# A hybrid streaming-encoder block on one core: heads spaced further apart, one gate projection moved ahead of the first norm, small blocks moved to GpSimd, weight sums pinned

## The chip, the core and the metric

The kernel runs on one core of a Trainium2 chip. The metric is the device time of one execution in microseconds (us). An engine's name in the profile stands for: PE the matrix engine TensorE (PEld its weight loads), DVE VectorE, ACT ScalarE, POOL GpSimd, SP SyncE, which here only starts transfers.

## What is computed

One layer of a hybrid block on 512 frames of 1024 channels, in float32:

```python
h = rmsnorm(x, norm1_w[l])
proj = h @ w_in[l]
q, k, v, z, b_raw, a_raw, glu, gates = jnp.split(proj, SPLITS, axis=-1)
...
beta = jax.nn.sigmoid(b_raw.astype(jnp.float32))
g = -jnp.exp(dn_A_log[l].astype(jnp.float32)) * jax.nn.softplus(
    a_raw.astype(jnp.float32) + dn_dt_bias[l].astype(jnp.float32))
o = gated_delta_rule_chunked(q, k, v, g, beta).astype(x.dtype)
o = rmsnorm(o, dn_norm_w[l]) * jax.nn.silu(z.reshape(B, T, DN_HEADS, DN_HEAD_DIM))
out_a = o.reshape(B, T, DN_WIDTH) @ dn_w_o[l]
...
c = causal_depthwise_conv(c, cm_dw_w[l]) + cm_dw_b[l]
c = jax.nn.silu(layernorm(c, cm_ln_w[l], cm_ln_b[l]))
out_b = c @ cm_w_pw2[l] + cm_b_pw2[l]
...
x = x + (gate_a * out_a + gate_b * out_b) @ w_out[l]
h2 = rmsnorm(x, norm2_w[l])
f_gate, f_up = jnp.split(h2 @ ffn_w_gate_up[l], 2, axis=-1)
x = x + (jax.nn.silu(f_gate) * f_up) @ ffn_w_down[l]
```

q, k and v go through a 4-tap causal convolution and silu, c is a gated linear unit followed by a 31-tap one, and the delta rule solves a triangular system in each chunk, for 8 heads of 128 channels.

## The kernel before

**Products.** Every weight arrives as float32 (`raw`) and is split in two: ScalarE rounds it to `whi` (L107) and VectorE subtracts to get `wlo` (L108). The data are split the same way (`hh` and `hl`, `yh` and `yl`, and so on). A product is then three matrix products, hh·whi, hl·whi and hh·wlo (`split3`, L117). A column unit of 128 columns takes 8 steps of k, 24 products of 512 columns. The 64 units of the input projection, and those of the later projections, pass through three weight buffers (`unit`, L97).

**Start.** SyncE starts the transfers one after another: the vectors `vec`, then quarter by quarter the inputs `xt` and quarters of three weight units, with the small weights of beta and alpha (`wba`, L228) behind the first inputs. The first three units (two for the first gated linear unit, one for the second) and the products for beta and alpha (L263, L264) are made from `uh` and `ul`, the input times the norm's weight, split, not yet divided by the root mean square. The result is multiplied by the reciprocal root, `rsb`, afterwards. Only then come the normalized `hh` and `hl` (L297, L298), on which all later projections work. VectorE then turns alpha into the decays `g` (L316 to L333), in small steps.

**Heads.** Python generators lay out the program. `step()` takes the next step from a queue of `head(h)` and `take(8)`: a head is its four projections k, q, v and z, one step for each k; `take` does eight steps of `others()`, the gated linear units and then the 16 gates. So heads are 40 steps apart. Besides, `chains` hold work that advances when the step count allows: `decays()` (the four matrix products L699 that sum g within chunks, and L706), each head's second half, and, from step 84 on every 40 steps, the chain of one head, in which small products, R (L547) and w (L552) go back and forth between TensorE, VectorE and ScalarE. `front(h)` prepares it: GpSimd multiplies `Un` by the decay `DT` (L420). The diagonal blocks of 32x32 are copied out as `cp` by ScalarE (four copies, L425), and combined to 16x16 blocks `cc` by ScalarE (L427) and VectorE (L428). `cc` is written to memory and read back spread out as `U`. GpSimd makes `Ud` (L437) and inverts the blocks in 15 rounds of two small instructions (L446, L448). `finish` (L589, L590) transposes a head's output and multiplies it by silu of z.

The 31-tap convolution is 240 VectorE instructions (L612) of low priority, emitted every 40 steps. `behind()` and `issue_after` hold an instruction back in its engine's order until marked ones of other work have been issued; within these rules a scheduler orders each engine's instructions.

**Fill work.** Sums of weight blocks for the feed-forward (Strassen-like products) are made beside the rest: transfers that accumulate, started by GpSimd, and GpSimd additions on halves of blocks (`dsums_add`, L167, in the tiles U, wsh, wst).

**After the heads.** The output projection splits the heads' results (L799, L800) and multiplies by `wo`. Within it stand the layer norm's mean (L631) and, three units later, its norm (L647). In between VectorE subtracts the mean, ScalarE squares and GpSimd adds the squares (L642). Then follow the point-wise projection, the merge and `w_out`, the second norm, and transposes of its result (L902) into hh and hl (L904, L905), 128 frames at a time. The first three feed-forward units begin with 256 of the 512 frames, before the last transposes (`norm2`, L886 to L892). Feed-forward up and down follow. In the down projection `two` (L1119) adds finished partial sums from a list `left`, one at each k.

## Time and profile before

| | us |
|---|---|
| median of three runs | 975.80 |
| lowest, highest | 973.53, 977.41 |
| the profiled execution | 975.02 |
| its span in the trace | 973.2 |
| TensorE busy | 942.7 |
| VectorE busy | 730.4 |
| ScalarE busy | 537.9 |
| GpSimd busy | 347.9 |

A row of the timeline gives start, duration, engine, line, operation, output and inputs, shape and count, and in brackets how long the engine was idle before it and what it then waited for. A row of waits gives engine, operation and releaser, then the total, the number and the longest of such waits. A row of a group gives busy time and mean length in ns, then the idle time before it. A row of windows gives the stretch, its length, and the busy time and number of instructions of PE, PEld, DVE, ACT and POOL, then the granted clock, the share of DMA and GB/s. Records of matrix products overlap, so the time that one takes is read from the distance of two starts.

### The profile page before, as it was taken

The page shows a single profiled execution, that of the slowest core. Times are in us where ns is not written, and L with a number is a line of the kernel's source. Part 1 is how long each engine was busy: PE and PEld are TensorE (multiplying, and loading weights), DVE is VectorE, ACT ScalarE, POOL GpSimd, SP SyncE. Part 2 cuts the span into 40 slices and gives each one's busy share as a digit, 9 for nine tenths or more (in the row PEclk, how much of TensorE's full clock was granted, in tenths as well). Part 3 has the DMA queues.
Part 4 walks back from the last instruction along what each step waited for, and adds up shares of the span by engine and source line. Part 5 has one row for each costly group of instructions (what it writes and reads, how often), then busy time and mean ns, then how long its engine had stood idle before and what let it go on. Part 6 is the DMA issues. An engine that isn't in the chain of part 4 may idle for free. (4 is left out here: it accounts for less than half of the span.)

```text
span 973.2 us, 14887 instructions
## 1 busy us (share of the span) xinstructions
PE 942.7 (97%) x5199; PEld 795.3 (82%) x5199; DVE 730.4 (75%) x1125; ACT 537.9 (55%) x1130; POOL 347.9 (36%) x516
## 2 busy tenths in 40 slices
PE   7999999999999999999998999999999999999996
PEld 5687878878787888888886888888889999988875
DVE  4898988878888868889667753666434787789775
ACT  6688768678767573543536332333323554556544
POOL 0314524424252345254253442254441111134225
PEclk9999999999999999999999999999999999999998
DMA  8233422313222247688987985488899656577654
GB/s 316 86 128 100 142 78 66 99 44 122 81 84 89 76 132 217 180 258 286 299 253 233 272 254 162 174 242 281 282 266 222 205 174 196 171 225 246 225 180 143
DMA packets 78300, 177.40 MB, mean 182 GB/s; under 512 B 10209, under 2 KB 19329, under 8 KB 77201
## 3 DMA queue, kind: packets, MB, share of 16 engines
q1 hardware_dynamic: 66816, 144.88, 44.7%
q0 software_dynamic: 10256, 28.89, 12.9%
q10 hardware_dynamic: 1152, 2.69, 0.7%
q8 instruction: 41, 0.67, 0.3%
q14 instruction: 35, 0.28, 0.1%
HBM read 156.22 MB, written 45.37 MB: 207 GB/s over the span
## 5 line engine op out<-in xcount | busy, mean ns | idle before, releaser
L107 ACT ACTIVATE whi<-raw 128x1024 fp32r<-128x1024 f32 (+1 forms) x191 | 196.2, 1029 | 253.4 <-PE mm L117 154.3
L108 DVE TENSOR_TENSOR wlo<-raw,whi 128x1024 fp32r<-128x1024 f32 (+1 forms) x191 | 239.6, 1255 | 93.8 <-ACT whi L107 92.7
L117 PE MATMUL mm<-hh,whi 128*128 128x512 f32 (+1 forms) x688 | 269.5, 392 | 0.0
L117 PE MATMUL mm<-hl,whi 128*128 128x512 f32 (+1 forms) x688 | 263.5, 383 | 2.3 <-POOL hl L298 1.7
L117 PE MATMUL mm<-hh,wlo 128*128 128x512 f32 (+1 forms) x688 | 264.7, 385 | 0.5 <-DVE wlo L108 0.5
L612 DVE SCALAR_TENSOR_TENSOR cps<-c,c31w,cps 128x512 f32<-128x512 f32 x240 | 180.0, 750 | 5.7 <-ACT cps L610 1.6
L117 PEld LDWEIGHTS mm<-hl,whi 128*128 128x128 f32 x688 | 129.9, 189 | 24.7 <-POOL hl L298 2.9
L117 PEld LDWEIGHTS mm<-hh,wlo 128*128 128x128 f32 x688 | 129.6, 188 | 24.3 <-DVE wlo L108 0.9
L117 PEld LDWEIGHTS mm<-hh,whi 128*128 128x128 f32 x688 | 129.8, 189 | 21.0 <-ACT hh L297 0.2
L939 POOL TENSOR_TENSOR fm<-fm 128x256 f32<-128x256 f32 x33 | 30.1, 914 | 113.7 <-DVE s L939 91.9
L446 POOL TENSOR_TENSOR ytm<-U,y 128x60 f32<-128x60 f32 (+14 forms) x120 | 37.4, 311 | 53.3 <-DMA U<-sc 39.0
L370 DVE SCALAR_TENSOR_TENSOR acc<-mm,c4w,acc 128x511 f32<-128x511 f32 (+2 forms) x72 | 53.0, 738 | 2.1 <-ACT acc L367 1.7
L117 PE MATMUL mm<-yh,whi 128*128 128x512 f32 x128 | 51.3, 401 | 0.0
L117 PE MATMUL mm<-yh,wlo 128*128 128x512 f32 x128 | 50.5, 395 | 0.0
L117 PE MATMUL mm<-yl,whi 128*128 128x512 f32 x128 | 50.3, 393 | 0.0
L117 PE MATMUL w<-hl,whi 128*128 128x256 f32 x168 | 47.5, 283 | 1.1 <-DVE hl L905 1.1
L117 PE MATMUL w<-hh,wlo 128*128 128x256 f32 x168 | 47.6, 284 | 0.8 <-DVE wlo L108 0.8
L117 PE MATMUL w<-hh,whi 128*128 128x256 f32 x168 | 47.3, 284 | 0.2 <-ACT hh L904 0.2
L117 PE MATMUL w<-wlo,fh 128*128 128x512 f32 (+1 forms) x115 | 44.5, 387 | 0.6 <-DVE wlo L108 0.6
L117 PE MATMUL w<-whi,fl 128*128 128x512 f32 (+1 forms) x115 | 44.2, 385 | 0.0
L117 PE MATMUL w<-whi,fh 128*128 128x512 f32 (+1 forms) x115 | 44.2, 384 | 0.0
L191 POOL DMA_DIRECT2D s<-in_wgu_dram x24 | 22.6, 957 | 54.4 <-DMA s<-in_wgu_dram 54.4
(320 smaller groups left out, 1912.5 us busy)
## 6 DMA issues: line engine op xcount, KB each, us to landing
raw<-in_win_dram SPq DMA_DIRECT2D x61, 512.0 KB, 3.5
raw<-in_wgu_dram SPq DMA_DIRECT2D x32, 512.0 KB, 3.6
s<-in_wgu_dram SPq DMA_DIRECT2D x48, 256.0 KB, 5.7
raw<-s SPq DMA_DIRECT2D x48, 256.0 KB, 3.5
raw<-wsum SPq DMA_DIRECT2D x44, 256.0 KB, 4.2
raw<-in_wdn_dram SPq DMA_DIRECT2D x33, 256.0 KB, 4.1
s<-in_wgu_dram POOLq DMA_DIRECT2D x24, 256.0 KB, 6.6
s<-s POOLq DMA_DIRECT2D x24, 256.0 KB, 6.6
```

The costliest lines, as they stand in the source:

```text
L107: marked(S.activation(hi, raw, AF.Copy), "unit")
L108: marked(V.tensor_tensor(out=lo, in0=raw, in1=hi.bitcast(F32), op=ALU.subtract), "unit")
L117: marked(PE.matmul(ps, l, r, start=first and i == 0, stop=last and i == 2))
L191: fed.append(nc.gpsimd.dma_start(*begun.pop(0), accum_op=ALU.add, max_dma_last_dim=2048))
L370: marked(V.scalar_tensor_tensor(out=acc[:, s:], in0=ps[:, :T - s], scalar=c4w[:, j, k:k + 1], in1=acc[:, s:], op0=ALU.mult, op1=ALU.add))
L446: G.tensor_tensor(out=tm[:, :, 0:w], in0=U[:, k, :, k + 1:], in1=y[:, :, k:k + 1].broadcast_to([P, NT, w]), op=ALU.mult)
L612: V.scalar_tensor_tensor(out=acc, in0=c[:, k:k + T], scalar=c31w[:, i, k:k + 1], in1=acc, op0=ALU.mult, op1=ALU.add)
L939: return eng.tensor_tensor(out=out, in0=in0, in1=in1, op=op)
```

## The change

The line numbers of the kernel after are 1 to 22 higher. The core of the diff:

```diff
+OTHERS = (12, 12, 12, 12, 8, 8, 8, 8)
...
     def dsums_add(k, r, cs=slice(0, T)):
...
+        with tc.issue_after(last[0].ins):
+            for o, x, y in ((b22, b12, b22), (b12, b11, b12), (b11, b22, b11), (b21, b11, b21)):
+                G.tensor_tensor(out=o, in0=x, in1=y, op=ALU.add)
...
-        nc.sync.dma_start(vec, a["vec"])
+        nc.scalar.dma_start(vec, a["vec"])
...
+            for u in (1, 2):
+                load(u, q)
             if q == 0:
                 nc.sync.dma_start(wb, a["wba"])
-            for u in (1, 2):
-                load(u, q)
...
+            if k == 1:
+                V.tensor_copy(out=wbh, in_=wb)
+                V.tensor_tensor(out=wbl, in0=wb, in1=wbh.bitcast(F32), op=ALU.subtract)
+            for b in [k - 2] if 1 < k < KD - 1 else [k - 2, k - 1, k] if k > 1 else []:
+                PE.matmul(bps[0:32, :], wbs[:, 32 * b:32 * b + 32], uh[:, b, :], start=b == 0, stop=False)
+                PE.matmul(bps[0:16, :], wbs[:, 32 * b:32 * b + 16], ul[:, b, :], start=False, stop=b == KD - 1)
...
+        zps = pst.tile([P, 4, P], F32, name="st").rearrange("p n t -> p (n t)")
+        hi, lo = unit(a["win"][24])
+        for k in range(KD):
+            c = slice(k * P, k * P + P)
+            split3(zps, (hi[:, c], lo[:, c]), uh[:, k, :], ul[:, k, :], k == 0, k == KD - 1)
...
+        with tc.issue_after(g_.ins):
+            V.tensor_tensor(out=zall[:, 0, :], in0=zps, in1=rsb, op=ALU.mult)
+        S.activation(zall[:, 0, :], zall[:, 0, :], AF.Silu)
...
-        DT = gp.tile([P, NT, P], F32, name="DT", bufs=2)
+        DT = gp.tile([P, NT, P], F32, name="DT", bufs=3)
...
-            S.copy(out=cp[b32], in_=Un[b32, :, b32])
...
+            (G.tensor_copy if h else S.copy)(out=cp[b32], in_=Un[b32, :, b32])
+        if h:
+            G.tensor_scalar(out=cc, in0=cp[:, :, 0:16], scalar1=mh1, scalar2=None, op0=ALU.mult)
+            G.tensor_scalar(out=cp[:, :, 0:16], in0=cp[:, :, 16:32], scalar1=mh2, scalar2=None, op0=ALU.mult)
+            c_ = G.tensor_tensor(out=cc, in0=cc, in1=cp[:, :, 0:16], op=ALU.add)
...
+        with tc.issue_after(c_.ins) if h else nullcontext():
+            G.tensor_tensor(out=Ud, in0=Un, in1=mc.rearrange("p (a t) -> p a t", a=1).broadcast_to([P, NT, P]),
+                            op=ALU.mult)
...
-            if count[0] % ROUND == 0:
+            if count[0] % 8 == 0:
                 background()
...
-        yield 2
+        yield 6
...
+        if h:
+            pz = yield from proj(24 + h)
+            S.activation(z_, pz, AF.Silu)
...
-        chains.append([count[0] + 5, second()])
+        chains.append([count[0] + (5 if h else 13), second()])
...
-        queue.append(take(8))
+        queue.append(take(OTHERS[h] if h else 8 + OTHERS[0]))
...
-        if nh < H and count[0] >= START + ROUND * nh:
+        if nh < H and count[0] >= START + 32 * nh + sum(OTHERS[:nh]):
...
-                for ps, w in first:
+                for ps, w in first[:2]:
                     k_loop(ps, w, slice(0, 2 * P))
-                transposes(3)
+                with tc.issue_after(transposes(3).ins):
+                    k_loop(*first[2], slice(0, 2 * P))
...
-            if left:
+            if left and k % 2:
                 with behind():
                     left.pop(0)()
```

In words. The vectors are loaded by ScalarE's queue, the small weights after the first three weight quarters, and the products for beta and alpha trail the projection by two steps of k. Head 0's z projection is made in the start stage from uh and ul, into the bank that the chains use later, and scaled by rsb behind g. Heads stand 44 steps apart four times, then 40; head 0 takes 20 steps of others in place of its z. The blocks of heads 1 to 7 are copied, scaled and added by GpSimd. The weight sums' additions stand behind the last of the small inversions, or of the squares' sums, that has been laid out before them (`last[0]`). The last transposes stand before the third of the half loops. In the down projection `left` is taken up at odd k only. The convolution's taps are emitted every 8 steps.

TensorE's order around the first normalized projections, before: `b` is the last early unit, `g<-cst,cv` the transposes of beta and alpha (L306), `mm<-hh` and `mm<-hl` the first normalized ones.

```order
L117 MATMUL b<-uh,whi 128x512
L117 MATMUL b<-ul,whi 128x512
L117 MATMUL b<-uh,wlo 128x512
L306 MATMUL g<-cst,cv 128x32 x4
L117 MATMUL mm<-hh,whi 128x512
L117 MATMUL mm<-hl,whi 128x512
L117 MATMUL mm<-hh,wlo 128x512
```

After, 24 products into the bank `st` stand between the two; here are the last of them.

```order
L118 MATMUL st<-uh,whi 128x512
L118 MATMUL st<-ul,whi 128x512
L118 MATMUL st<-uh,wlo 128x512
L318 MATMUL g<-cst,cv 128x32 x4
L118 MATMUL mm<-hh,whi 128x512
L118 MATMUL mm<-hl,whi 128x512
```

The decays' products (L699, now L719) come 90 products behind L306 in before, and 59 behind L318 in after.

TensorE's order where the heads end, before: the transposes of head 7's output (`b<-cst,o`) are followed by further gates' products.

```order
L117 MATMUL mm<-hh,wlo 128x512
L383 MATMUL b<-cst,o 128x128 x4
L117 MATMUL mm<-hh,whi 128x512
L117 MATMUL mm<-hl,whi 128x512
L117 MATMUL mm<-hh,wlo 128x512
```

After, the output projection's (`yh`, `yl`) follow at once, with the layer norm's mean (L651) among the first.

```order
L118 MATMUL mm<-hh,wlo 128x512
L397 MATMUL b<-cst,o 128x128 x4
L118 MATMUL mm<-yh,whi 128x512 x2
L651 MATMUL mm<-sacc,cst 128x512
L118 MATMUL mm<-yl,whi 128x512
L118 MATMUL mm<-yh,wlo 128x512
```

Of the 72 products between transposes and output projection none is left; between mean and norm there are now 119 where there were 73.

GpSimd's order around the squares' sums (`sacc`), before: a weight sum in the tile `wsh` and its transfer stand ahead.

```order
L167 TENSOR_TENSOR wsh<-wsh 128x256 x4
L168 DMA wsum<-wsh 512x1x256
L191 DMA s_127<-s_125 128x512
L642 TENSOR_TENSOR sacc<-sacc,acc_5220 128x512
L642 TENSOR_TENSOR sacc<-sacc,acc_5224 128x512
```

After, the first `wsh` sum stands behind the last square.

```order
L193 DMA s_125<-s_124 128x512
L662 TENSOR_TENSOR sacc<-sacc,acc_5221 128x512
L662 TENSOR_TENSOR sacc<-sacc,acc_5225 128x512
L662 TENSOR_TENSOR sacc<-sacc,acc_5229 128x512
L662 TENSOR_TENSOR sacc<-sacc,acc_5233 128x512
L662 TENSOR_TENSOR sacc<-sacc,acc_5237 128x512
L662 TENSOR_TENSOR sacc<-sacc,acc_5241 128x512
L662 TENSOR_TENSOR sacc<-sacc,acc_5245 128x512
L193 DMA s_124<-in_wgu_dram 128x512
L169 TENSOR_TENSOR wsh<-wsh 128x256 x4
```

More of the change, by code (lines that the diff above doesn't have):

```diff
@@ L165, in dsums_add @@
         b11, b12, b21, b22 = (r[:, i, :] for i in range(4))
-        for o, x, y in ((b22, b12, b22), (b12, b11, b12), (b11, b22, b11), (b21, b11, b21)):
-            G.tensor_tensor(out=o, in0=x, in1=y, op=ALU.add)
+        with tc.issue_after(last[0].ins):
+            for o, x, y in ((b22, b12, b22), (b12, b11, b12), (b11, b22, b11), (b21, b11, b21)):
+                G.tensor_tensor(out=o, in0=x, in1=y, op=ALU.add)
         nc.gpsimd.dma_start(wsum[k][:, :, cs], r)
@@ L243, in block_kernel @@
         wbh, wbl = wbhl[:, :, 0, :], wbhl[:, :, 1, :]
-        V.tensor_copy(out=wbh, in_=wb)
-        V.tensor_tensor(out=wbl, in0=wb, in1=wbh.bitcast(F32), op=ALU.subtract)
         bps = psg.tile([P, T], F32, name="g")
@@ L262, in block_kernel @@
                 split3(ps, (hi[:, c], lo[:, c]), uh[:, k, :], ul[:, k, :], k == 0, k == KD - 1)
-            PE.matmul(bps[0:32, :], wbs[:, 32 * k:32 * k + 32], uh[:, k, :], start=k == 0, stop=False)
-            PE.matmul(bps[0:16, :], wbs[:, 32 * k:32 * k + 16], ul[:, k, :], start=False, stop=k == KD - 1)
+            if k == 1:
[4 more added lines that the diff above has]
+                PE.matmul(bps[0:16, :], wbs[:, 32 * b:32 * b + 16], ul[:, b, :], start=False, stop=b == KD - 1)
         ss = st.tile([P, 2, NT], F32, name="rms_ss", bufs=1)
@@ L281, in block_kernel @@
             split3(eps_[3], (hi[:, c], lo[:, c]), uh[:, k, :], ul[:, k, :], k == 0, k == KD - 1)
+        zps = pst.tile([P, 4, P], F32, name="st").rearrange("p n t -> p (n t)")
[3 more added lines that the diff above has]
+            split3(zps, (hi[:, c], lo[:, c]), uh[:, k, :], ul[:, k, :], k == 0, k == KD - 1)
+        zall = pa_.tile([P, H, T], F32, name="A")
         def glu0(i):
@@ L332, in block_kernel @@
         V.scalar_tensor_tensor(out=sp, in0=ax, scalar=0.0, in1=sp, op0=ALU.max, op1=ALU.add)
-        V.tensor_tensor(out=g, in0=sp, in1=nea.rearrange("p (a h) -> p a h", a=1).broadcast_to([P, NT, H]),
+        g_ = V.tensor_tensor(out=g, in0=sp, in1=nea.rearrange("p (a h) -> p a h", a=1).broadcast_to([P, NT, H]),
                         op=ALU.mult)
@@ L375, in conv4 @@
         return o
-    zall = pa_.tile([P, H, T], F32, name="A")
     junk = tp.tile([P, T], F32, name="pa", bufs=1)
@@ L422, in front @@
         cp = gp.tile([P, NT, 32], F32, name="cp")
+        cc = gp.tile([P, NT, 16], F32, name="cc")
         for b in range(4):
             b32 = slice(32 * b, 32 * b + 32)
-            S.copy(out=cp[b32], in_=Un[b32, :, b32])
-        cc = gp.tile([P, NT, 16], F32, name="cc")
-        S.activation(cc, cp[:, :, 0:16], AF.Copy, scale=mh1)
-        V.scalar_tensor_tensor(out=cc, in0=cp[:, :, 16:32], scalar=mh2, in1=cc, op0=ALU.mult, op1=ALU.add)
+            (G.tensor_copy if h else S.copy)(out=cp[b32], in_=Un[b32, :, b32])
[3 more added lines that the diff above has]
+            c_ = G.tensor_tensor(out=cc, in0=cc, in1=cp[:, :, 0:16], op=ALU.add)
+        else:
+            S.activation(cc, cp[:, :, 0:16], AF.Copy, scale=mh1)
+            V.scalar_tensor_tensor(out=cc, in0=cp[:, :, 16:32], scalar=mh2, in1=cc, op0=ALU.mult, op1=ALU.add)
         sc = dram.tile([8, 16, NT, 16], F32, name="sc")
@@ L436, in front @@
         Ud = gp.tile([P, NT, P], F32, name="Ud", bufs=3)
-        G.tensor_tensor(out=Ud, in0=Un, in1=mc.rearrange("p (a t) -> p a t", a=1).broadcast_to([P, NT, P]),
-                        op=ALU.mult)
+        with tc.issue_after(c_.ins) if h else nullcontext():
+            G.tensor_tensor(out=Ud, in0=Un, in1=mc.rearrange("p (a t) -> p a t", a=1).broadcast_to([P, NT, P]),
+                            op=ALU.mult)
         y = gp.tile([P, NT, 16], F32, name="y", bufs=3)
@@ L728, in head @@
         v_ = yield from v
-        pz = yield from proj(24 + h)
         z_ = zall[:, h, :]
-        S.activation(z_, pz, AF.Silu)
+        if h:
+            pz = yield from proj(24 + h)
+            S.activation(z_, pz, AF.Silu)
         def second():
@@ L901, in transposes @@
                     k = 4 * j + c
-                    PE.transpose(ps[:, c, :], xs2[:, n, k * P:(k + 1) * P], ident)
+                    t = PE.transpose(ps[:, c, :], xs2[:, n, k * P:(k + 1) * P], ident)
             k4 = slice(4 * j, 4 * j + 4)
             S.activation(hh[:, k4, ts], ps, AF.Copy)
-            V.tensor_tensor(out=hl[:, k4, ts], in0=ps, in1=hh[:, k4, ts].bitcast(F32), op=ALU.subtract)
+            marked(V.tensor_tensor(out=hl[:, k4, ts], in0=ps, in1=hh[:, k4, ts].bitcast(F32), op=ALU.subtract), "hl")
+        return t
     first = []
```

## The prediction

> **What bounds the kernel now.** I read the page's busy times first, then TensorE's waits by releaser, then the timeline around each wait.

> ```profile
> PE 942.7 (97%) x5199; PEld 795.3 (82%) x5199; DVE 730.4 (75%) x1125; ACT 537.9 (55%) x1130; POOL 347.9 (36%) x516
> ...
> PE mm L647 <- POOL sacc L642: 3.5, 1, 3.5
> PE st L555 <- ACT w L552: 3.2, 4, 1.1
> ...
> PE g L383 <- ACT Vp L456: 1.0, 1, 1.0
> PE st L550 <- DVE R L547: 1.0, 1, 1.0
> ```

> TensorE is busy 97% of the 973.2 us span: it is the bound, and every other engine matters only where TensorE waits for it. The rows behind the first give total, number and longest of such waits. The change takes no matrix product away, so the most it can win is waiting and slow clock. Two pairs of neighbouring rows give the price of a 512-column product at either clock, as the distance of their starts:

> ```profile
> 506.42 0.39 PE L117 MATMUL mm<-yh,wlo 128*128 128x512 f32 x1
> 506.65 0.39 PE L117 MATMUL mm<-yh,whi 128*128 128x512 f32 x1
> ...
> 518.17 0.63 PE L117 MATMUL mm<-yh,whi 128*128 128x512 f32 x1
> 518.60 0.63 PE L117 MATMUL mm<-yl,whi 128*128 128x512 f32 x1
> ```

> So 0.23 us at the full clock (0.2275 over longer rows) and 0.43 at the slow one. I sum against the profiled execution, 975.0 us (its span and 1.8 around it); the runs' median, 975.8, lies 0.8 above it.

> **1. Start: −1.1 us (−0.7 to −1.5).**

> ```profile
> 0.73 0.39 SPq L216 DMA_DIRECT2D vec<-in_vec_dram  x1
> 1.17 0.42 SPq L224 DMA_DIRECT2D xt<-in_xt_dram  x1
> ...
> 7.07 0.61 PE L263 MATMUL g<-uh,cv 128*32 128x512 f32 x1 [7.07 <-DVE cv L245]
> ```

> The first product is one of beta/alpha, and it waits for the small weights' split. With vec on ScalarE's queue SyncE issues every input one slot (0.44 us) earlier, and the first product becomes one of the projection, which needs only xt and a weight quarter. Both rows together say it can start at about 5.95 instead of 7.07. The small weights come in behind the quarters, and their products trail by two k, so nothing waits for them. The lower end is the slot alone and some of the DVE step, the upper one has the weight quarter a slot earlier as well.

> **2. Un-normalized gate ahead of the normalized inputs: −3.0 (−2.5 to −3.9).**

> ```profile
> 36.00:46.00 10.00, 7.68 (x31) 5.03 (x31) 9.94 (x13) 4.56 (x8) 6.02 (x4) 1.00 0.00 0
> ...
> 40.37 0.50 PE L117 MATMUL mm<-hl,whi 128*128 128x512 f32 x1 [1.29 <-POOL hl L298]
> 45.32 0.50 PE L117 MATMUL mm<-hl,whi 128*128 128x512 f32 x1 [0.36 <-POOL hl L298]
> ```

> Between 36 and 46 us TensorE issues 31 products, 31 × 0.2275 = 7.05 us of work in 10: 2.95 lost waiting for hh and hl, which DVE (9.94 of 10 busy) makes no faster. Head 0's z now fills 24 × 0.2275 = 5.46 us ahead of it. The last hl, used at 45.3, is ready a microsecond earlier (its chain starts with part 1) and wanted at about 45.5, so none of these waits stays. The upper end leaves the 0.36; the lower adds what falls outside the window. The z products are no extra: they leave head 0's later steps.

> **3. A new wait in its place, at the decay products: +2.6 (0 to +4.3).** They stood behind 90 products of the first projections, and now stand behind 59. The window is DVE's from the first step behind hl to g (L333), which they need:

> ```profile
> 44.95:59.98 15.03, 14.67 (x65) 12.12 (x65) 13.95 (x33) 12.38 (x18) 2.72 (x9) 1.00 0.34 113
> ...
> L370 DVE SCALAR_TENSOR_TENSOR acc<-mm,c4w,acc 128x511 f32<-128x511 f32 (+2 forms) x8 | 5.8, 719 | 0.2 <-ACT acc L367 0.2
> L108 DVE TENSOR_TENSOR wlo<-raw,whi 128x1024 fp32r<-128x1024 f32 x4 | 4.9, 1220 | 0.2 <-ACT whi L107 0.2
> L612 DVE SCALAR_TENSOR_TENSOR cps<-c,c31w,cps 128x512 f32<-128x512 f32 x3 | 2.2, 744 | 0.0
> ...
> 59.88 0.18 DVE L333 TENSOR_TENSOR cv<-cv 128x32 f32<-128x32 f32 x1
> 60.45 0.97 PE L699 MATMUL g<-cv,cst 128*128 128x32 f32 x8
> ```

> The first projection starts at about 36.1 − 1.1 + 5.5 = 40.5, so TensorE is at the decays at 40.5 + 59 × 0.2275 = 53.9. DVE comes to the window's start 1.1 earlier, at 43.85. Of its 13.95 us of work it now does, ahead of g, three 4-tap steps and one split less and two 31-tap steps more: 13.95 − 3 × 0.72 − 1.22 + 2 × 0.74 = 12.05. That is 55.9, with g itself 56.1, and 0.4 from its end to TensorE (60.06 to 60.45): TensorE starts them at 56.5, 2.6 late. All projections of head 0 queue behind, so this is lost outright. The high end adds the window's own idle time, 1.1, and as much again of the 12.38 ScalarE is busy with; the low end is DVE in time.

> **4. 16x16 blocks on GpSimd: −5.0 (0 to −6.5).** Around one of the six waits of the heads' chains (the three last rows of the first fence: 3.2 + 1.0 + 1.0 = 5.2 us):

> ```profile
> 259.96 1.22 ACT L425 COPY cp<-Un 32x128 f32<-32x128 f32 x4 [0.63 <-POOL Un L420]
> ...
> 262.21 0.28 DVE L428 SCALAR_TENSOR_TENSOR cc<-cp,cst,cc 128x64 f32<-128x64 f32 x1 [1.37 <-ACT cc L427]
> 262.81 0.49 PE L550 MATMUL st<-R,Y 128*128 128x128 f32 x2 [0.98 <-DVE R L547]
> ...
> L446 POOL TENSOR_TENSOR ytm<-U,y x120: 208/256/1314, 87.6 to 365.0; 128x60 f32<-128x60 f32 x8, 128x56 f32<-128x56 f32 x8, 128x52 f32<-128x52 f32 x8, 128x48 f32<-128x48 f32 x8
> ```

> ScalarE stops for GpSimd's Un, copies, and DVE stops 1.37 us for ScalarE; behind them in both queues stand another head's chain steps, R and w, and TensorE waits for these. With the blocks on GpSimd neither queue stops there. I take 5.0 of the 5.2; the low end adds the fill and drain around each, the high end is that the queues stop for something else. GpSimd pays 7 heads × 7 instructions × 0.3 us (the row's median is 0.26 for the nearest size) = 15 us, hidden: it is 36% busy. Its own pinning of Ud delays nothing TensorE asks for soon. The wider spacing (44 steps four times, then 40) and the third decay buffer move products among each other at no price, ±1.

> **5. The end of head 7: +1.8 (+1.0 to +5.5).**

> ```profile
> 466.53 0.60 PE L383 MATMUL b<-cst,o 128*128 128x128 f32 x4
> 467.17 0.75 DVE L590 SCALAR_TENSOR_TENSOR A<-b,vec,A 128x512 f32<-128x512 f32 x1
> 467.84 1.21 DVE L108 TENSOR_TENSOR wlo<-raw,whi 128x1024 fp32r<-128x1024 f32 x1
> 469.50 4.28 ACT L799 ACTIVATE yh<-A 128x512 fp32r<-128x512 f32 x8 [1.36 <-issue]
> 470.16 4.90 DVE L800 TENSOR_TENSOR yl<-A,yh 128x512 fp32r<-128x512 f32 x8 [1.11 <-ACT yh L799]
> ```

> Before, 72 products (16.4 us) stand between head 7's transposes and the first product of the output projection. The later chains leave none: two yh products, the layer norm's mean, then one with yl. From the transposes at T the order gives L590 at T + 0.65, the split to T + 2.5, the first yl to T + 3.1. TensorE is there at T + 0.36 + 0.46 + 0.5 = T + 1.3: 1.8 us of waiting. Then DVE's 0.61 a yl (4.90 / 8) keeps ahead of 3 × 0.2275 a k. If the 1.36 of idle ScalarE returns, 3.6 are lost, and the slow clock can follow (next part), hence the high end.

> **6. The norm of the layer norm: −5.5 (−3.7 to −5.9).**

> ```profile
> 496.77 4.35 POOL L167 TENSOR_TENSOR wsh<-wsh 128x256 f32<-128x256 f32 x4 [0.33 <-DMA wsh<-in_wdn_dram]
> 502.68 12.32 POOL L642 TENSOR_TENSOR sacc<-sacc,acc 128x512 f32<-128x512 f32 x7
> 511.18 0.39 PE L117 MATMUL mm<-yh,wlo 128*128 128x512 f32 x1
> 515.05 1.12 PE L647 MATMUL mm<-sacc,cst 128*128 128x512 f32 x2 [3.48 <-POOL sacc L642]
> ```

> GpSimd adds weight sums (4.35) ahead of the seven squares (12.3), and TensorE stands from 511.4 to 515.05, 3.65 us. The rows of 518 us, after it, are at the slow pitch: nine products × 0.2 = 1.8 more. The change pins the weight adds behind the squares and puts 27 us of products (119, not 73) between mean and norm. The squares are added once part 5's eight yl are split, from about T + 9, and take 12.3, to T + 21; TensorE comes to the norm at T + 1.3 + 1.8 + 27 = T + 30. So 3.65 + 1.8 are gone; the high end keeps the slow clock. [...]

> **7. The last transposes before the feed-forward: −1.8 (−1.0 to −2.6).**

> ```profile
> 633.61 1.04 PE L902 MATMUL mm<-cst,xs 128*128 128x128 f32 x8
> 634.89 0.62 PE L117 MATMUL w<-hh,whi 128*128 128x256 f32 x3 [0.25 <-ACT hh L904]
> 636.62 0.39 PE L117 MATMUL w<-hl,whi 128*128 128x256 f32 x1 [1.10 <-DVE hl L905]
> ```

> From 634.5 (eight transposes at 0.11) to 636.62 TensorE does three products of 0.12: 1.8 lost. Now the third half loop, 24 × 0.12 = 2.9 us, lies between, longer than the 2.1 that hh and hl take; and xs, in time already, isn't asked for too early. The ends are 0.8 either way, a split's wait that comes or goes with the new order.

> **8. Down projection: −0.9 (0 to −0.9).**

> ```profile
> 928.52 2.31 DVE L108 TENSOR_TENSOR wlo<-raw,whi 128x1024 fp32r<-128x1024 f32 x1
> 930.89 0.50 PE L117 MATMUL w<-wlo,fh 128*128 128x512 f32 x1 [0.62 <-DVE wlo L108]
> ```

> Sums that are taken up at every second k only leave DVE time for the split that TensorE waits for.

> **Sum:** −1.1 − 3.0 + 2.6 − 5.0 + 1.8 − 5.5 − 1.8 − 0.9 = −12.9. That is 962.1 for the profiled execution and, 0.8 above, 963 for the median. A measurement of this kernel tells some 0.5% (4.9 us) from no change.

> **Rivals.** *More is won:* g and yl come in time (parts 3 and 5 at 0 and +1) and the chains' waits go with their seams (−6.5): −12.9 − 2.6 − 0.8 − 1.5 = −17.8, 958. For it: my DVE sum of part 3 is rough. [...] *The chains' waits stay:* the queues are late for other reasons, as conv4 and conv31 fill DVE; −7.9, 968. Against it: the 1.37 stop stands right ahead of R. *The change doesn't do what it says:* norm, chains and stalls all on the bad side, −12.9 + 5.0 + 5.5 + 5.4 = +3.0, 979.

> *Slower:* GpSimd and DVE stand in each other's way in the heads' stage. The split of part 8 took 2.31 us beside GpSimd's adds, and 1.21 at 467.84 without. If the small GpSimd instructions took 1.3 us (the long end of L446's row) instead of 0.3, each head would hold 7 × 1.3 = 9.1 us; with a third of that on TensorE, 3 us a head, 7 × 3 − 7.9 = +13, 989. It decides from 1.8 us a head (4.9 + 7.9 over 7). Against it:

> ```profile
> L612 DVE SCALAR_TENSOR_TENSOR cps<-c,c31w,cps x113: 719/755/757, 301.3 to 476.1; 128x512 f32<-128x512 f32 x113
> ```

> [...]

> **How the numbers follow.** Forecast 0.57, more won 0.10, high stalls 0.13, waits stay 0.12, not as it says 0.04, slower 0.04. Low 955 is three below the case in which more is won, for parts 2 and 7 at their low ends (−0.9, −0.8) and the starts of the others; high 972 takes in the two cases at 968 with their spread. Faster is below 970.9: 0.57 + 0.10, and 0.21 of the 0.25 at 968, 0.88; same 0.08; slower 0.04.

> **What would show it.** First product near 5.95 us; no wait for hl at L117; a wait of 2 to 3 us at the decays; no ACT copies of cp after head 0 and no R or w waits of 1 us; a wait of 1.8 for yl, clock full; none at the norm and none for hl at 636. I am wrong if the heads' stage keeps its 5 us or either new stall passes 3.4.

## The result, and the profile after

The kernel after takes 965.9 us (median of five runs, 965.64 to 966.77), the kernel before 975.8 (973.53 to 977.41): a ratio of 0.9904, with a 95% interval of 0.9887 to 0.9922. That is 9.9 us less; 12.9 were forecast. The profiled execution's span is 964.0 us, 9.3 less than before.

The rows that answer to those shown of before, first the busy times, then TensorE's waits by releaser (total, number, longest):

```profile
PE 941.0 (98%) x5199; PEld 796.0 (83%) x5199; DVE 739.3 (77%) x1119; ACT 527.0 (55%) x1095; POOL 361.6 (38%) x561
...
PE mm L118 <- ACT whi L258: 6.0, 1, 6.0
PE g L719 <- issue: 1.9, 1, 1.9
PE w L118 <- DVE wlo L109: 1.7, 5, 0.5
PE mm L118 <- issue: 1.6, 1, 1.6
PE mm L118 <- DVE wlo L109: 1.4, 2, 0.7
PE b L526 <- DVE Xd L514: 0.8, 1, 0.8
PE g L397 <- ACT vT L388: 0.6, 1, 0.6
PE st L564 <- DVE o L589: 0.4, 1, 0.4
PE st L575 <- ACT w L572: 0.4, 1, 0.4
```

Of the old list (norm 3.5, w 3.2, R 1.0, Vp 1.0, hl 2.3 together) nothing over 0.4 is left. In its place stand two new waits that the forecast had (the decays, L719, and the first product of the output projection, 1.6) and one that it did not have: `wlo`, 3.1 us in seven waits, where it had been 2.1 in five at other places. The waits of 0.8, 0.6 and 0.4 for Xd, vT and o, in the heads, are new and small.

To see where the time went I take for each stage TensorE's lost time: the distance of the starts of two neighbouring records, less the usual distance of that form. In brackets is what lies in pieces over 0.3 us, that is, in real waits; the rest lies in smaller pieces, or is slow clock. Such a piece is the 0.09 us where a 64-column product follows a 512-column one in before: 0.32 from start to start (123.53 to 123.85 us) instead of 0.23. "Again" is a second profiled execution of the same kernel (the run after_again below).

| stage | before | after | again |
|---|---|---|---|
| first product at | 7.07 | 6.04 | 6.05 |
| start, to the first normalized product | 2.5 | 2.3 | 2.8 |
| from there to the decays | 3.8 (2.8) | 2.3 (2.1) | 2.3 (2.1) |
| 7 us from the decays on | 0.3 | 1.8 | 1.8 |
| heads | 40.9 (8.1) | 36.1 (3.1) | 36.5 (3.4) |
| last transposes of the heads, first wo products | 0.0 | 2.7 (2.3) | 2.7 (2.3) |
| rest of wo and wpw, with the norm | 6.4 (4.8) | 0.7 (0.4) | 0.7 (0.4) |
| second norm and its transposes | 3.9 (2.9) | 1.5 (0.5) | 1.5 (0.5) |
| feed-forward up | 0.7 (0.4) | 4.1 (3.3) | 1.7 (1.2) |
| down | 1.4 (0.8) | 0.8 (0.4) | 0.8 (0.4) |

**The start.** The timeline of after: the inputs are issued one slot earlier, and a product of the projection is the first.

```profile
0.73 0.39 SPq L226 DMA_DIRECT2D xt<-in_xt_dram  x1
...
6.04 0.80 PE L118 MATMUL mm<-uh,whi 128*128 128x512 f32 x1 [6.04 <-ACT whi L258]
```

**The decays.** The windows around them (stretch, length, busy PE, PEld, DVE, ACT, POOL, then the granted clock), and the timeline:

```profile
40.31:53.80 13.49, 13.49 (x61) 10.99 (x59) 13.49 (x29) 9.43 (x13) 1.76 (x2) 1.00 0.24 78
53.80:57.20 3.40, 1.47 (x11) 1.11 (x10) 3.25 (x8) 0.69 (x4) 0.61 (x2) 1.00 0.46 159
57.20:61.40 4.20, 4.20 (x12) 3.31 (x12) 3.58 (x6) 3.47 (x8) 1.81 (x7) 0.59 0.21 57
...
55.61 0.18 DVE L345 TENSOR_TENSOR cv<-cv 128x32 f32<-128x32 f32 x1
55.89 1.05 PE L719 MATMUL g<-cv,cst 128*128 128x32 f32 x8 [1.93 <-issue]
57.71 0.63 PE L118 MATMUL mm<-hh,whi 128*128 128x512 f32 x1
58.14 0.63 PE L118 MATMUL mm<-hl,whi 128*128 128x512 f32 x1
```

The first window is full: all waits for hh and hl are gone. In the second TensorE waits for g, which is ready at 55.79, and does ten small products. (The profile names no releaser for this wait, `issue`; the products start 0.1 us behind g.) In the third the granted clock is 0.59, and 512-column products are 0.43 apart. The forecast had the wait (2.6 forecast, 2.1 measured), but not the slow clock behind it.

**The norm.** GpSimd's squares come ahead of the weight sums, and the norm's product (L667) waits for nothing:

```profile
487.42 11.67 POOL L662 TENSOR_TENSOR sacc<-sacc,acc 128x512 f32<-128x512 f32 x7 [5.93 <-ACT acc L661]
502.30 4.10 POOL L169 TENSOR_TENSOR wsh<-wsh 128x256 f32<-128x256 f32 x4
507.32 1.02 PE L667 MATMUL mm<-sacc,cst 128*128 128x512 f32 x2
```

**The last transposes** are followed by a product at once (621.59, and no wait in the rows behind it):

```profile
620.80 1.04 PE L923 MATMUL mm<-cst,xs 128*128 128x128 f32 x8
621.59 0.36 PE L118 MATMUL w<-hh,whi 128*128 128x256 f32 x1
621.79 0.28 PE L118 MATMUL w<-hl,whi 128*128 128x256 f32 x1
```

**The feed-forward stage**, where nothing was forecast. Timeline and one window:

```profile
720.36 7.13 POOL L169 TENSOR_TENSOR wst<-wst 128x512 f32<-128x512 f32 x4 [6.75 <-DMA wst<-in_wdn_dram]
737.42 1.06 ACT L108 ACTIVATE whi<-raw 128x1024 fp32r<-128x1024 f32 x1 [4.52 <-DMA raw<-s]
738.51 1.23 DVE L109 TENSOR_TENSOR wlo<-raw,whi 128x1024 fp32r<-128x1024 f32 x1 [3.56 <-ACT whi L108]
739.79 0.39 PE L118 MATMUL mm<-th,wlo 128*128 128x256 f32 x1 [0.74 <-DVE wlo L109]
...
727.00:757.00 30.00, 27.92 (x226) 27.10 (x225) 17.56 (x25) 10.61 (x15) 9.29 (x12) 1.00 0.97 256
```

ScalarE waits 4.5 us for a Strassen sum to arrive (`raw<-s`), VectorE for ScalarE, TensorE for VectorE. The DMA engines are busy to 0.97 there; the same place of before:

```profile
736.00:766.00 30.00, 29.78 (x242) 29.31 (x241) 20.12 (x29) 13.14 (x20) 4.84 (x6) 1.00 0.80 214
```

After makes five whole weight sums (wst) in this stage where before makes four, since the feed opens at step 335 and the program has fewer steps left then, as head 0's eight z steps are gone: seven U halves, five wsh halves and five whole blocks, instead of eight, six and four.

### The profile page after: what moved, and what is told of

It reads as the page before. It is cut to its first block, busy times and chain, and to the rows that moved or that the text cites. A ratio compares the mean times of both kernels' runs of the same rounds, so it can differ in the third digit from the quotient of the medians.

```text
span 964.0 us, 14861 instructions
## 1 busy us (share of the span) xinstructions
PE 941.0 (98%) x5199; PEld 796.0 (83%) x5199; DVE 739.3 (77%) x1119; ACT 527.0 (55%) x1095; POOL 361.6 (38%) x561
## 4 chain that ended last, share of the span: by engine, by line
PE 86%; DVE 5%; DMA 3%; ACT 2%; issue 2%; POOL 2%; POOLq 0%; ACTq 0%; DVEq 0%; SPq 0%
PE mm L118 58%; PE w L118 18%; DMA raw<-s 2%; PE g L397 1%; DVE wlo L109 1%; PE st L576 1%; DVE xt L307 1%; PE b L508 1%; PE st L570 1%; PE g L430 1%; DMA raw<-in_wgu_dram 1%; PE st L575 1%; PE b L502 1%; PE g L479 1%; POOL ss L891 1%
## 5 line engine op out<-in xcount | busy, mean ns | idle before, releaser
L108 ACT ACTIVATE whi<-raw 128x1024 fp32r<-128x1024 f32 (+1 forms) x191 | 196.5, 1030 | 247.9 <-PE mm L118 151.8
L109 DVE TENSOR_TENSOR wlo<-raw,whi 128x1024 fp32r<-128x1024 f32 (+1 forms) x191 | 245.5, 1287 | 94.5 <-ACT whi L108 93.3
L118 PE MATMUL mm<-hh,whi 128*128 128x512 f32 (+1 forms) x680 | 266.1, 391 | 0.1
L118 PE MATMUL mm<-hh,wlo 128*128 128x512 f32 (+1 forms) x680 | 262.0, 386 | 0.6 <-DVE wlo L109 0.6
L118 PE MATMUL mm<-hl,whi 128*128 128x512 f32 (+1 forms) x680 | 260.8, 384 | 0.0
L169 POOL TENSOR_TENSOR wst<-wst 128x512 f32<-128x512 f32 x20 | 34.0, 1699 | 31.3 <-DMA wst<-in_wdn_dram 30.1
```

The costliest lines, as they stand in the source:

```text
L108: marked(S.activation(hi, raw, AF.Copy), "unit")
L109: marked(V.tensor_tensor(out=lo, in0=raw, in1=hi.bitcast(F32), op=ALU.subtract), "unit")
L118: marked(PE.matmul(ps, l, r, start=first and i == 0, stop=last and i == 2))
L169: G.tensor_tensor(out=o, in0=x, in1=y, op=ALU.add)
```

## The experiments

Twelve runs; each has its own runs of the kernel before on the same chip (medians 974.9 to 975.1).

**The feed opened earlier** (feed_early).

```diff
-        start_feed[0] = count[0] >= 335
+        start_feed[0] = count[0] >= 328
```

> The kernel after with the weight sums' feed opened at step 328 instead of 335, so that eight U halves, six wsh halves and four whole wst blocks are made as before the change, instead of seven, five and five. Theory (the fifth whole block, added by GpSimd in the feed-forward stage and 2 MB of transfers with it, holds up the Strassen sums that TensorE's weights come from): the waits between 738 and 760 us, 3.3 us, go, and the time falls from 965.9 to about 962.5. Rival (these waits come from the order of that stage itself): no change, 965 to 967.

Measured: 963.75 us (962.18 to 964.75), ratio 0.9879 (0.9864 to 0.9893). In the profile the stage falls from 4.1 us lost to 0.6, with no piece over 0.3, span 961.5. Its window:

```profile
730.00:760.00 30.00, 29.97 (x250) 29.77 (x249) 20.78 (x31) 13.41 (x19) 4.21 (x6) 1.00 0.77 208
```

The stage's waits come from the fifth block: in the seven profiled executions with five blocks the stage loses 1.2 to 5.5 us in pieces, in the seven with four 0.0 to 1.3. Whether the block's transfers or GpSimd's additions weigh more was not separated; the chain of waits shown above starts at a transfer. By the ratios the edit is worth 2.4 us (0.9904 to 0.9879, with intervals that just overlap), less than the profile's 3.5: as the column "again" shows, this stage's price in after differs from execution to execution.

The same on the kernel before, the other way round (before_late_feed): step 345 instead of 335, which makes seven, five and five there.

> The kernel before with the weight sums' feed opened at step 345 instead of 335, so that it makes seven U halves, five wsh halves and five whole wst blocks, as after does; all else as before. Theory (the fifth whole block holds up the Strassen sums): TensorE's lost time in the feed-forward stage, 0.7 us in before, rises to 3 or 4 us, with waits for wlo between 740 and 775. Rival (the waits belong to after's order): it stays below 1 us.

Measured: one execution, 975.86 us, span 974.0. The feed-forward stage loses 6.2 us (5.5 in pieces) instead of 0.7; the window there:

```profile
736.00:766.00 30.00, 27.14 (x225) 26.73 (x224) 17.14 (x25) 10.54 (x15) 8.98 (x11) 1.00 1.00 263
```

So the theory holds on both kernels. But the span hardly moved, which I had not expected: the norm's stage lost 2.6 instead of 6.4. With one wsh sum less GpSimd starts the squares at 498.2 instead of 502.7; the norm waits 0.8 instead of 3.5, and no slow clock follows. The work that is put off costs later what it gave before.

**The blocks back on ScalarE and VectorE** (blocks_back): the four copies, scale and add of L440 to L447 without the branch for GpSimd, Ud not pinned.

```diff
-            (G.tensor_copy if h else S.copy)(out=cp[b32], in_=Un[b32, :, b32])
+            S.copy(out=cp[b32], in_=Un[b32, :, b32])
```

> The kernel after with the 16x16 blocks of all heads copied by ScalarE and combined by ScalarE and VectorE, as before; all else as after. Theory (the blocks in the two queues made the heads' chains wait): pieces of TensorE's waiting over 0.3 us in the heads' stage rise from 3.1 to about 8 us, and the time to 970 or 971. Rival (the wider spacing of the heads removed the waits): they stay near 3, time 965 to 967.

Measured: 970.42 us (967.07 to 973.33), ratio 0.9957 (0.9941 to 0.9973). The heads' stage has 8.1 us in pieces again, against 3.1, and the waits for w and R are back:

```profile
PE st L570 <- ACT w L567: 2.0, 3, 1.2
...
PE st L565 <- DVE R L562: 1.7, 2, 1.0
```

**Only the blocks, on the kernel before** (before_blocks), with the scalings, the add and the place of Ud as in after; its first line:

```diff
-            S.copy(out=cp[b32], in_=Un[b32, :, b32])
+            (G.tensor_copy if h else S.copy)(out=cp[b32], in_=Un[b32, :, b32])
```

> The kernel before with only the 16x16 blocks of heads 1 to 7 moved to GpSimd. Theory (the blocks alone make the heads' waits): pieces of waiting over 0.3 us in the heads' stage fall from 8.1 to about 3, span 973.2 to about 968. Rival (they need the spacing too): they stay above 6.

Measured: one execution, 973.58 us, span 971.4; pieces in the heads' stage 4.8 us, between the two expectations. The waits for w and R fall from 4.2 us to 1.1, as the theory has it, but the first chain has a new one:

```profile
PE b L494 <- ACT Q L490: 1.9, 1, 1.9
...
PE st L561 <- ACT w L558: 0.8, 2, 0.5
```

After has no such wait. Which of its other edits prevents it wasn't tried. So the blocks alone bring 3.3 of the 5.0 us. The span fell by 1.8 only, not by 5: among other things the granted clock is 0.50 for 6.8 us behind the norm's wait here, where it was for 3.4 in before.

**Heads 40 steps apart** (spacing_8).

```diff
-OTHERS = (12, 12, 12, 12, 8, 8, 8, 8)
+OTHERS = (8, 8, 8, 8, 8, 8, 8, 8)
```

> The kernel after with eight steps of others behind every head, as before, instead of twelve for the first four: the last chain ends earlier and 50 products come between head 7's transposes and the output projection; 73 instead of 119 between mean and norm. Theory: the stall at the output projection's start, 2.1 us, goes; the heads' waits stay low, as the blocks are on GpSimd; the squares are still added ahead of the weight sums, so the norm's wait stays gone: about 964. Rival (the spacing is what removed the heads' waits, or the 119 products what removed the norm's): 3 to 5 us come back, 967 to 970.

Measured: 965.21 us (963.12 to 966.73), ratio 0.9894 (0.9876 to 0.9911): the same as after. The stall at the output projection's start is gone (2.7 to 0.0), the heads keep 2.3 in pieces, so the spacing didn't remove their waits: there the theory holds. Its 964 isn't met, since the rest of wo loses 2.3 (the norm's product itself waits 0.2), and feed-forward 6.0 in this execution, against 4.1. Of the 6.0 some 1.7 are slow clock (0.50 from 739.7 to 743.1), and the stage differs between executions of after itself, so that part can't be put down to the spacing. What the spacing trades is the stall at the heads' end for one in the rest of wo; the wider spacing of the change won nothing that can be measured.

**The same without the pin** (spacing_8_pinless): the additions of the weight sums are free.

```diff
-        with tc.issue_after(last[0].ins):
+        with nullcontext():
```

> The run with eight steps behind every head, and the weight sums' additions no longer pinned: in GpSimd's order three wsh sums then stand before or among the squares. Between mean and norm lie 73 products, as before the change. Theory (the pin is worth what stands in GpSimd's way, the distance the rest): the wait at the norm, 1.8 us with the pin, grows to 6 us or more with the slow clock behind it. Rival (the distance alone decides): 1.8 us as with the pin.

Measured: one execution, 965.37 us, no slower than with the pin, as feed-forward lost 2.8 us less in it. The norm waits 3.3 us instead of 0.2, with the slow clock behind it for 3.4 us, and its stage loses 6.3 instead of 2.3. GpSimd does two wsh additions first, and others between the squares:

```profile
491.47 2.93 POOL L169 TENSOR_TENSOR wsh<-wsh 128x256 f32<-128x256 f32 x2
494.36 1.29 POOL L662 TENSOR_TENSOR sacc<-sacc,acc 128x512 f32<-128x512 f32 x1
495.61 0.73 POOL L169 TENSOR_TENSOR wsh<-wsh 128x256 f32<-128x256 f32 x1
...
506.53 1.98 PE L667 MATMUL mm<-sacc,cst 128*128 128x512 f32 x2 [3.26 <-POOL sacc L662]
```

So at 73 products between mean and norm the pin is what counts in this stage. After itself, with 119, was not run without the pin; what the pin does there is not shown.

**Head 0's z back in its steps** (no_z): the 24 products into `st`, their scaling and silu are taken out, head 0 makes z like the others and takes 12 steps of others.

```diff
-        if h:
-            pz = yield from proj(24 + h)
-            S.activation(z_, pz, AF.Silu)
+        pz = yield from proj(24 + h)
+        S.activation(z_, pz, AF.Silu)
```

> The kernel after with head 0's z projection back in its own steps, on the normalized inputs; all else as after. This also moves the decays behind more products, brings back 20 products between head 7's transposes and the output projection, and makes four whole weight blocks in the feed-forward stage again. Theory (each of these has its own price): the waits for hh and hl return, +3.6; the decays' wait with the slow clock after it goes, -3.8; the stall at the end of the heads goes, -2.1; the feed-forward waits go, -3.3: together -5.6, about 960. Rival (the move of z is worth what it was forecast to be, and the others do not hang on it): about 968 to 970.

Measured: 962.63 us (962.04 to 964.14), ratio 0.9873 (0.9857 to 0.9890), span 959.7: faster than after by 3 us, by the ratios; the interval touches that of after and lies clear of that of after_again (0.9895 to 0.9931). The waits for hh and hl are back (3.7 lost to the decays), but the wait at the decays, the slow clock, the stall at the heads' end and the feed-forward waits (0.3 lost) are all gone; the norm's stage costs 1.9 more, which I hadn't counted. The move of z does what it is for, and costs more than it wins.

**The decays behind 72 products** (decay_late), by a lower priority for the four products.

```diff
+        prio = tc.cur_priority
+        tc.cur_priority = prio + 160
         for i, m in enumerate((tri, suf, ones, mid)):
             PE.matmul(gps[:, i, 0:32], m, fl(g), start=True, stop=True)
...
         PE.matmul(mps[0:32, 0, :], fl(g), mid, start=True, stop=True)
+        tc.cur_priority = prio
```

> The kernel after with the four decay products given a lower priority, so that they stand behind 72 products of the first projections instead of 59; all else as after. In after TensorE waited 2.1 us for them (g came at 55.8) and the products behind them then ran at the slow clock until 60.9 (granted clock 0.60). Theory (wait and slow clock come from their place alone): both go, -2.1 and -1.7, the time falls from about 965.5 to 961.5 or 962. Rival (the slow clock comes from the ten small products, not from the wait): only the 2.1 go and the granted clock stays near 0.6 behind them, about 963.5.

Measured: 963.91 us (962.76 to 964.36), ratio 0.9886 (0.9866 to 0.9905). The wait and the slow clock are both gone; the same ten products now cost nothing that shows:

```profile
53.50:57.00 3.50, 3.50 (x17) 2.92 (x16) 3.50 (x10) 1.35 (x2) 0.11 (x1) 1.00 0.47 150
57.00:60.50 3.50, 3.50 (x21) 2.38 (x21) 3.46 (x5) 3.10 (x7) 2.28 (x8) 1.00 0.21 64
```

The clock of 1.00 speaks against the rival, though the time is the rival's. By the ratios the edit is worth 1.8 us (with intervals that overlap), half of what the theory's sum had; in the profiled execution feed-forward loses 6.3 us, 2.2 more than in after, which takes the other half. Of these, 1.7 are slow clock again: behind a wait of 2.0 us for a Strassen sum's `whi` the granted clock is 0.50 from 750.8 to 754.2. Why that wait is longer here, in a stage 690 us later that still has its fifth block, wasn't tried.

**All three together**, with twelve steps behind two heads (combo_12_12), behind none (combo_8), or as in after (combo_keep), and after once more. The three have the diffs of feed_early and decay_late, and their own `OTHERS`.

> The kernel after with three changes: feed opened at step 328, decay products behind 72 products, and twelve steps of others only behind the first two heads, then eight, which puts 25 products between head 7's transposes and the output projection. Theory (the prices add up): -3.5 in the feed-forward stage, -3.8 at the decays, -2.6 at the output projection's start, +1.5 at the norm, where 73 products are left: -8.4, about 957. Rival (they trade with each other through VectorE and GpSimd): 960 to 963.

> The kernel after with feed opened at step 328, decay products behind 72 products, and eight steps of others behind every head (49 products between head 7's transposes and the output projection). Theory (prices add): like the run with twelve steps behind two heads, nothing lost at the output projection's start, 2.3 at the norm, under 0.6 in the feed-forward stage, span 956 to 957, median 960 to 962. Rival (the spacing of the first heads matters by itself): 2 us or more apart from that run.

> The kernel after with feed opened at step 328 and decay products behind 72 products, and the heads' spacing as in after. Theory: the stall at the output projection's start stays at 2.6, the norm loses 0.7 to 1.8, so it lies within 1.5 us of the run with eight steps behind every head, which loses 0 and 2.3 there. Rival (the wide spacing costs or wins by itself): over 2 us apart.

> The kernel after once more, unchanged, for a second profiled execution on the chip of the two runs below. If the slow clock behind the decays' wait and the feed-forward waits are fixed by the program, its profile shows 1.8 us lost behind the decays and 4.1 in the feed-forward stage again; if they hang on where a clock window or a transfer falls, either differs by a microsecond or more with the same instructions. Time 964 to 967.

Measured:

| run | median (range) | ratio (95%) | span | heads' end | norm's stage | feed-forward |
|---|---|---|---|---|---|---|
| after_again | 965.99 (963.81 to 969.30) | 0.9913 (0.9895 to 0.9931) | 962.5 | 2.7 | 0.7 | 1.7 |
| combo_12_12 | 961.57 (958.42 to 962.50) | 0.9867 (0.9844 to 0.9889) | 956.2 | 0.0 | 2.4 | 0.3 |
| combo_8 | 959.28 (958.86 to 961.93) | 0.9844 (0.9829 to 0.9860) | 959.4 | 0.0 | 4.0 | 1.8 |
| combo_keep | 962.44 (959.75 to 965.15) | 0.9872 (0.9855 to 0.9889) | 960.0 | 2.6 | 2.9 | 0.3 |

after_again has the slow clock behind the decays once more (1.8), so that price came back, but not feed-forward's (1.7 instead of 4.1). combo_8 beats both kernels: 6.7 us below after on the same chip, 15.6 below before. For its median the expectation was missed by 0.7 us; its profiled execution is the slowest of its four and loses 1.8 in feed-forward, where under 0.6 was expected, with four whole blocks. combo_8 lies 2.3 below combo_12_12 by the medians, as its rival had it, but the intervals overlap, so which spacing is better stays open. For combo_12_12 the sum (957) was nearly met by the profiled execution (958.4, the fastest of its four); the median, 961.6, missed it by 4.6 us and lies in the range of the rival, by which the three prices do not simply add. combo_keep lies 3.2 above combo_8, which speaks for its rival, with intervals that overlap.

## Why the prediction was right, and where it was off

The direction, the range and most steps held; the median came 2.9 us above the forecast. Parts 2, 4 and 6 have runs that take the cause away (no_z, blocks_back, and spacing_8_pinless at another spacing); parts 1, 7 and 8 are read from the traces of before and after alone. By its parts, from the table of lost time:

1. Start: −1.0 (forecast −1.1). The first product came at 6.04 us, as worked out from the slot of the queue and the weight quarter.
2. hh and hl: −3.6 (−3.0), the whole loss of that stretch, as its lower end had it.
3. Decays: +2.1 for the wait (+2.6) and +1.5 for the slow clock, which was not in the sum. The working of the wait was right: TensorE there at 53.8 (53.9), g at 55.8 (56.1). Its high end was not: 1.1 and as much again make +4.8, not +4.3. No run shows 3.4 us, or another length, as the wait from which the clock falls. What the runs showed: 1.9 us of waiting with small products behind it was followed by a granted clock of 0.59; before's wait of 1.29 at 40.37 left it at 1.00; and in the 3.41 us of before that end where its clock falls behind the norm's wait (513.05 to 516.46) TensorE was still busy for 1.41. The chance of 0.13 for high stalls has parts 3 and 5 both at their high ends (+1.7 and +3.7 over the forecast, 968); measured were waits of 1.9 and 1.6, with the lower clock behind the first alone.
4. Blocks on GpSimd: −5.0 in pieces (−5.0). blocks_back shows the cause: all of it comes back without them. They are not the whole of it, since on the kernel before the blocks alone brought 3.3. GpSimd's price was 22 us, not 15. By their medians (copies 0.29 us, scalings 0.45, add 0.32) the 49 instructions would take 16.5; seven of them took 1.1 to 1.3 us, each beside a split of VectorE of 1.2 to 1.3. So the long instructions of the slower rival did occur, seven times, but no wait of TensorE in this stage names GpSimd. The new wait for Xd (0.8 us) comes behind two of VectorE's small copies (median 0.24 us) that took 0.60 and 0.79 while GpSimd's weight sums ran, at 407 to 410 us; whether these lengthened them was not tried. The row of L612 that stands against that rival, 719 to 757 ns in 113 instructions (301 to 477 us of before, GpSimd busy for 74.6 of 175.6), speaks for this one form; of other forms nothing was shown there.
5. End of the heads: +2.7 (+1.8). The first yl product started at T + 3.2 (forecast T + 3.1), but the wait stood ahead of it: ScalarE's split to yh began at T + 1.5 only, so the first yh product waited 1.6, which the sum had let start at once. The clock stayed full. The 3.6 at the high end does not follow from its terms: 1.8 and 1.36 make 3.2.
6. Norm: −5.7 (−5.5). The squares were done at 499.1, 8 us early (forecast 9). The prediction names both the pin and the distance. spacing_8 keeps the wait away with the pin and 73 products, spacing_8_pinless does not; what the distance of 119 would do alone was not run.
7. Last transposes: −2.4 (−1.8), also the waits around them that I had left to the range.
8. Down: −0.6 (−0.9).

The term that is missing: +3.4 us in the profiled execution (+1.0 in the second) in feed-forward up. The step that failed is the one that has the z products as "no extra": head 0's eight z steps are gone, and fewer steps after the feed opens mean one whole weight block more in a stage where the DMA engines are already at 0.80. The wider spacing has no part in it: spacing_8, without it, still makes five whole blocks, and no_z, with it, makes four. Before's trace showed the four blocks and the 0.80; the program of after makes five.

The two terms that the sum did not have, this one and the slow clock, come to 4.9 us in the profiled execution. Of the others, parts 2, 3 (the wait), 6 and 7 came out 1.9 us better than forecast, and 1, 5 and 8 1.3 worse. That the errors of the single parts nearly cancel is luck, not precision.

## What to carry to other kernels

A step that is taken out of a planned order shortens everything that is counted in steps: look up what starts at a fixed count (here the feed, the chains), and where the work that no longer fits will run. Moving 24 products in front of a wait of 3.6 us was right for that wait, and still lost, by no_z, through what was planned behind it. Work moved between engines is best judged by the waits of the step that queued behind it, not by the engine's share.

## What the runs showed of the hardware

In after the granted clock fell (0.59 over the next 4.2 us) behind a stretch of 3.4 us in which TensorE was busy 1.47 by the profile: 1.9 of waiting, then ten products of 32 and 128 columns. It did so in three of the six profiled executions with this same wait (0.59 in after and after_again, 0.60 in spacing_8); in feed_early, blocks_back and spacing_8_pinless it stayed at 1.00. Of these one, feed_early, is shown here:

```profile
55.20:58.70 3.50, 1.58 (x13) 1.14 (x11) 3.34 (x9) 0.80 (x4) 0.65 (x2) 1.00 0.45 150
58.70:62.90 4.20, 4.20 (x25) 3.57 (x24) 3.67 (x7) 4.17 (x12) 1.78 (x7) 1.00 0.27 69
```

The wait at the heads' end of after, with 1.8 us of work in 3.4, left the clock at 1.00:

```profile
476.90:480.30 3.40, 1.78 (x10) 1.22 (x8) 2.75 (x4) 3.40 (x6) 0.60 (x1) 1.00 0.96 318
480.30:484.00 3.70, 3.70 (x17) 2.84 (x16) 3.70 (x7) 2.86 (x6) 0.84 (x1) 1.00 0.98 322
```

```profile
53.92:57.33 3.41, 1.48 (x12) 1.23 (x12) 3.25 (x9) 0.70 (x5) 0.74 (x3) 1.00 0.46 159
57.33:60.74 3.41, 3.41 (x9) 2.63 (x10) 3.38 (x6) 3.34 (x7) 1.68 (x7) 0.50 0.12 19
...
53.35:56.76 3.41, 2.08 (x10) 1.38 (x8) 3.41 (x9) 2.36 (x3) 0.00 (x0) 1.00 0.23 60
56.76:60.17 3.41, 2.82 (x16) 2.34 (x17) 3.25 (x8) 1.71 (x5) 2.12 (x8) 1.00 0.26 100
```

In before and after four windows of this grid at the full clock are followed by a drop, and TensorE was busy for 1.00 to 1.51 us in each of them (1.41 and 1.51 in before, 1.48 and 1.00 in after). In every other one it was busy for at least 1.79, which is the window of the wait at the heads' end of after, 477.17 to 480.58. So a wait of 1.9 us, in a window with 1.48 us of work, was followed by a clock of 0.50 for 3.41 us in after; in feed_early the same wait, spread over windows with 2.08 and 2.82 us of work, was not. That the place of the grid makes this difference fits these rows; by itself it was not tried.
